# A hybrid attention and recurrent trunk in float32 pairs: gate products, weight casts and the last turn of the recurrent layer rearranged

## The chip, the cores and the metric

The kernel runs on one core of one Trainium2 chip. The metric is the device time of one execution in microseconds (us), as the median of several runs.

## The reference

The reference is an encoder trunk of two layers over 1040 tokens (16 meta tokens and 1024 of the sequence) of width 1024. Layer 0 is attention with a SiLU gate; the change leaves it alone. Layer 1 is recurrent, and it is where everything here happens:

```
zp = rms_norm(h) @ w_in;  u, gate = split(zp)        # 2048 columns each
xc = conv_b + sum(up[tap:tap+T] * conv_w[tap] for tap in 0..3)
for each direction (forward, backward):
    r = sigmoid(xc @ w_a + b_a);  i = sigmoid(xc @ w_x + b_x)     # 16 blocks of 128 x 128
    log_a = -8 * r * softplus(-lam);  a = exp(log_a)
    b = sqrt(1 - exp(2 * log_a)) * i * xc
    h_t = a_t * h_(t-1) + b_t
y = (forward + backward) * silu(gate);   out = h + y @ w_out
```

## The kernel before

**Number format.** Every matrix product is made of three: each operand is held as a rounded part ("hi", fp32r) and a remainder ("lo"), and lo times hi, hi times lo and hi times hi are added in PSUM. For a weight, `split_w` loads the raw 128x512 tile (SP's queue, tile wr, 3 buffers), makes the rounded half on GpSimd (line 106, tile wh) and the remainder on GpSimd (line 107, tile wl; 4 buffers of each). These three are issued at a priority 200 instructions ahead of where they stand. The weights of the recurrent gates have tiles of their own (wown).

**The recurrent layer.** Rows of the 2048 channels are cut into 16 blocks of 128 channels, one turn of the loop for each (line 1300, e = 0 to 15). Three blocks are in work in one turn: `cur` is projected (three chunks `u_chunk` of 346 to 348 columns and two chunks `g_chunk` of 512, each of 24 matmuls), `prev` has its four gate products (`gate(d, j)`: direction d, j = 0 for r and 1 for i; 9 matmuls for d = 0 and 6 for d = 1), its decays and its square root, and `late` has its two scans and is stored to HBM (s_y for the rounded part, s_yl for the remainder). PSUM has three single banks for the chunks (tag c), one tile of three banks (big, gates of d = 0) and one of two (two, gates of d = 1).

The names in the profile: pu and pg are the chunks' PSUM tiles, pz those of the gate products; ou the projected row, oxc the convolved row (lines 1166 to 1169), oxh and oxl its two halves (lines 758, 759); tz the tanh of r, then the decay's root; oz the tanh of i, then i times xc, then the recurrence's input and its result; oa the decay; og the half gate argument, otg its SiLU; oyh and oyl the halves of y.

**Order.** The framework's scheduler turns the program's order into one in-order queue for each engine, by priorities and an estimate of its own of when operands are ready. So the text order below is a wish and not the queue.

**After the loop.** The last block's gates and scans are finished, blocks 0 to 13 of y are read back from HBM (`y_load`, lines 1283 and 1284, two transfers of 512 KB for a block), and the output product runs over 8 tiles of 128 rows (d), each in four quarters of the 16 blocks (`o_part(d, qd)`, 24 matmuls of 512 columns, PSUM tile oo). Tiles 0, 1 and 2 are accumulated at the same time; the others one after another.

Of the kernel before, what the change touches and what calls it, by code (L numbers as in the profile page):

```python
# [10 lines left out]
AF = mybir.ActivationFunctionType  # L11
ALU = mybir.AluOpType
# [5 lines left out]
T = 1040  # L18
NM = 16
# [22 lines left out]
def trunk_kernel(ctx: ExitStack, tc: tile.TileContext, a: dict, out: bass.AP):  # L42
# [51 lines left out]
    def split_w(src, shape, nm, own=None, eng=nc.gpsimd, own_bufs=1):  # L94
        n = 1
        for s in shape:
            n *= s
        raw = wpool.tile([P, 512], F32, tag="wr", name="wr", bufs=3)
        if own:
            hi, lo = [sb["P"].tile([P, 512], F32R, tag=own + z, name="wown", bufs=own_bufs) for z in "hl"]  # L100
        else:
            hi = wpool.tile([P, 512], F32R, tag="wh", name="wh", bufs=4)
            lo = wpool.tile([P, 512], F32R, tag="wl", name="wl", bufs=4)
        with tc.high_priority(sb.get("ahead", 200)):
            nc.sync.dma_start(raw[:, :n], src)
            eng.tensor_scalar(hi[:, :n], raw[:, :n], 1.0, 1.0, ALU.mult, ALU.mult)  # L106
            eng.tensor_sub(lo[:, :n], raw[:, :n], hi[:, :n].bitcast(F32))  # L107
        if len(shape) == 2:
            f = lambda t: t[:, :n].rearrange("p (k m) -> p k m", k=shape[0])
        else:  # L110
            f = lambda t: t[:, :n]
        return f(hi), f(lo)
# [1033 lines left out]
    class Lru:  # L1146
# [25 lines left out]
            self.c = split(self.xc, "ox", "X")  # L1172

        def g_in(self, c, t):
            if c == 0:
                self.og = row("og", "T")
            nc.vector.scalar_tensor_tensor(self.og[:, 512 * c:512 * c + 512], t, 0.5, rstd[:, CHR[c][0]:CHR[c][1]],
                                           ALU.mult, ALU.mult)

        def g_chunk(self, c, w):  # L1180
            t = bank("pg", "c")
            chunk_mm(w, (0, 1), t, *CHR[c])
            self.g_in(c, t)

        def g_last(self, w):

            ts = [bank("pg", "c") for _ in range(2)]
            for hf in range(2):
                for c in range(2):
                    chunk_mm(w, (hf,), ts[c], *CHR[c])  # L1190
            for c in range(2):
                self.g_in(c, ts[c])

        def silu(self):
            og = self.og
            tg = self.tg = row("otg", "T")
            nc.scalar.activation(tg[:, :1024], og[:, :1024], AF.Tanh)
            nc.vector.scalar_tensor_tensor(tg[:, :1024], tg[:, :1024], 1.0, og[:, :1024], ALU.add, ALU.mult)

        def weights(self):  # L1200
            self.w = w_gates(self.e)
# [1 line left out]
        def gate(self, d, j):  # L1203
# [9 lines left out]
            mm3(ps, P, [(gh[:, 2 * d + j], gl[:, 2 * d + j], *self.c)], ch, off, True, True)  # L1213
            if j == 0 and d == 0:
                self.tz = sb["P"].tile([P, 2, T], F32, tag="tz", name="tz", bufs=2)
            z = self.tz[:, d] if j == 0 else row("oz", "X")
            bc = hb[:, 32 * j + 16 * d + e:32 * j + 16 * d + e + 1]
            nc.scalar.activation(z[:, :n], src, AF.Tanh, scale=0.5, bias=bc)
            if j == 1:
                self.z[d] = z  # L1220
                nc.vector.scalar_tensor_tensor(z[:, :n], z[:, :n], 1.0, self.xc[:, T - n:T], ALU.add, ALU.mult)

        def decay(self, d):

# [21 lines left out]
        def scan(self, d):  # L1246
            ti, av, n = self.z[d], self.av[d], T if d == 0 else T - NM
            if d == 0:
                nc.vector.tensor_tensor_scan(ti, av, ti, 0.0, ALU.mult, ALU.add)
            else:  # L1250
                nc.vector.tensor_tensor_scan(ti[:, :n][:, ::-1], av[:, :n][:, ::-1], ti[:, :n][:, ::-1], 0.0,
                                             ALU.mult, ALU.add)
                nc.gpsimd.tensor_add(ti[:, :1024], self.z[0][:, NM:T], ti[:, :1024])  # L1253

        def gated(self):
            yv = self.z[1]
# [42 lines left out]
    w_u = w2_load(0, 1)  # L1299
    for e in range(16):  # L1300
        cur = Lru(e)
        w_g = w2_load(e, 0)
        if e == 0:
            raw = [bank("pu", "c") for _ in range(3)]
# [21 lines left out]
        else:  # L1326
# [2 lines left out]
            cur.u_chunk(0, w_u)  # L1329
            if late:  # L1330
                late.scan(0)
            prev.gate(0, 0)
            prev.decay(0)
            cur.u_chunk(1, w_u)
            if late:
                late.scan(1)
            prev.gate(1, 0)
            prev.decay(1)
            cur.u_chunk(2, w_u)
            cur.conv()  # L1340
            prev.root()
            prev.gate(0, 1)
            if e < 15:
                w_u = w2_load(e + 1, 1)
            if late:
                late.gated()
            if e < 15:
                cur.g_chunk(0, w_g)
                cur.split_xc()
                prev.gate(1, 1)  # L1350
                cur.g_chunk(1, w_g)
            else:
                prev.gate(1, 1)
                cur.split_xc()
                cur.g_last(w_g)
            if late:
                late.store()
        cur.silu()
        cur.weights()
        late, prev = prev, cur  # L1360

    def pair_of(nm):
        ts = [bank(nm, "c") for _ in range(2)]
        return [(ts[j], 512 * j, 512 * j + 512) for j in range(2)]

    for e in range(4):
        y_load(e, "H")
    late.drive()
    late.scan(0)
    for d in range(2):  # L1370
        prev.gate(d, 0)
    for d in range(2):
        prev.gate(d, 1)
    for d in range(2):
        prev.decay(d)
    prev.root()
# [5 lines left out]
        y_load(e, "H")  # L1382
    late.store()
    prev.finish()
    o_part(0, 1, acc[0])
    for d in (1, 2):
        o_part(d, 0, acc[d])
    for e in range(8, 14):
        y_load(e, "X")
    for d in (1, 2):  # L1390
        o_part(d, 1, acc[d])
    for qd in range(2, 4):
        for d in range(3):
            o_part(d, qd, acc[d])
            if qd == 3:
# [109 lines left out]
```

## Time and profile before

| | us |
|---|---|
| median of 3 runs | 1940.13 |
| lowest and highest run | 1939.22, 1945.82 |
| the profiled execution | 1936.07 |
| span of its instructions | 1934.3 |
| TensorE busy in the span | 1828.5 |
| VectorE busy | 1278.4 |
| ScalarE busy | 827.9 |
| GpSimd busy | 943.9 |
| granted clock of TensorE, mean | 0.986 |

PE is TensorE's matmuls, PEld its weight loads, DVE is VectorE, ACT ScalarE, POOL GpSimd and SP the engine whose queue issues the transfers. Times of a window are counted from the first instruction. The recurrent loop's matmuls lie between about 1238 and 1725 us, what follows the loop between 1725 us and the end. An engine's busy time in a stretch has its waits left out; the clock is TensorE's granted share of full speed.

### The profile page before, as it was taken

How to read it: one execution, taken by the hardware profiler on the slowest of the kernel's cores; microseconds unless marked ns; L12 is line 12 of the kernel's file. 1: busy time of each engine (PE TensorE's matmuls, PEld its weight loads, DVE VectorE, ACT ScalarE, POOL GpSimd, SP SyncE). 2: the span in 40 equal slices, each digit the busy share in tenths (PEclk: the TensorE clock that was granted, in tenths of full speed). 3: DMA queues.
4: the chain of work that ended last, by engine and by line, in shares of the span. 5: the costliest groups of instructions: out<-in, count | busy, mean ns of one | idle time of the engine just before them, and what ended most of it. 6: DMA issues, size and time to landing. Idle time of an engine off the chain costs nothing.

```text
span 1934.3 us, 28455 instructions
## 1 busy us (share of the span) xinstructions
PE 1828.5 (95%) x10822; PEld 1659.4 (86%) x10822; DVE 1278.4 (66%) x1953; ACT 827.9 (43%) x1366; POOL 943.9 (49%) x780
## 2 busy tenths in 40 slices
PE   8999989998999999999999999999999899988999
PEld 7988988888999999788878999988888788876887
DVE  7686358787663432889888753368898989893000
ACT  5455224444342201666666642155656464652000
POOL 5455355535224652544433333358676777655331
PEclk9999999999999999999999999999999999998999
DMA  5256532222223451323221014312222222246521
GB/s 180 73 184 232 132 84 65 64 75 72 78 75 122 143 194 57 113 73 92 69 70 55 18 47 160 106 50 71 82 67 81 84 69 88 66 157 232 183 82 44
DMA packets 111062, 192.77 MB, mean 100 GB/s; under 512 B 32143, under 2 KB 51727, under 8 KB 110926
## 3 DMA queue, kind: packets, MB, share of 16 engines
q1 hardware_dynamic: 110926, 190.96, 31.4%
q8 instruction: 85, 1.39, 0.3%
q14 instruction: 51, 0.42, 0.1%
HBM read 129.86 MB, written 53.06 MB: 95 GB/s over the span
## 4 chain that ended last, share of the span: by engine, by line
PE 53%; DVE 20%; POOL 9%; issue 9%; DMA 5%; ACT 4%; SPq 1%; DVEq 0%; ACTq 0%; POOLq 0%
PE pj L159 10%; PE oo L159 8%; PE pxop L159 6%; PE px L918 4%; PE av L998 4%; PE op L159 3%; PE up L159 3%; PE tp L982 3%; PE vps L426 2%; DVE tz L1243 2%; DMA wr<-in_wg 2%; POOL oz L1253 2%; POOL wl L107 2%; DVE oxc L1167 2%; PE pg L1143 2%
## 5 line engine op out<-in xcount | busy, mean ns | idle before, releaser
L106 POOL TENSOR_SCALAR wh<-wr 128x512 fp32r<-128x512 f32 (+2 forms) x219 | 196.3, 897 | 396.4 <-PE pj L159 99.0
L107 POOL TENSOR_TENSOR wl<-wr,wh 128x512 fp32r<-128x512 f32 (+2 forms) x219 | 352.6, 1610 | 17.5
L159 PE MATMUL pj<-xh,wl 128*128 128x346 f32 (+1 forms) x768 | 251.8, 328 | 12.3 <-DVE wl L107 7.2
L159 PE MATMUL pj<-xl,wh 128*128 128x346 f32 (+1 forms) x768 | 249.3, 325 | 0.7 <-DVE xl L260 0.6
L159 PE MATMUL pj<-xh,wh 128*128 128x346 f32 (+1 forms) x768 | 248.9, 324 | 0.0
L159 PEld LDWEIGHTS pj<-xh,wl 128*128 128x128 f32 x768 | 146.6, 191 | 14.2 <-ACT xh L259 7.1
L159 PEld LDWEIGHTS pj<-xl,wh 128*128 128x128 f32 x768 | 146.7, 191 | 2.2 <-DVE xl L260 2.1
L159 PEld LDWEIGHTS pj<-xh,wh 128*128 128x128 f32 x768 | 146.6, 191 | 0.1
L936 POOL TENSOR_SCALAR mpm<-p,mmx 128x96 f32<-128x96 f32 (+1 forms) x69 | 25.7, 372 | 209.2 <-DVE mmx L931 119.9
L1143 PE MATMUL pu<-h1h,wl 128*128 128x346 f32 (+1 forms) x384 | 125.5, 327 | 0.8 <-POOL wh L106 0.8
L1143 PE MATMUL pu<-h1l,wh 128*128 128x346 f32 (+1 forms) x384 | 124.9, 325 | 0.0
L1143 PE MATMUL pu<-h1h,wh 128*128 128x346 f32 (+1 forms) x384 | 124.8, 325 | 0.0
L988 ACT CAST pth<-tp 128x512 fp32r<-128x512 f32 (+1 forms) x160 | 78.9, 506 | 83.4 <-PE tp L982 82.0
L1294 DVE TENSOR_TENSOR hres<-oo,hres 128x512 f32<-128x512 f32 x16 | 10.6, 687 | 151.6 <-PE oo L159 151.6
L989 DVE TENSOR_TENSOR ptl<-tp,pth 128x512 fp32r<-128x512 f32 (+1 forms) x160 | 91.9, 583 | 23.3 <-ACT pth L988 21.7
L159 PE MATMUL oo<-oyl,wh 128*128 128x512 f32 x256 | 102.3, 400 | 4.4 <-DMA oyl<-s_yl 4.4
L159 PE MATMUL oo<-oyh,wl 128*128 128x512 f32 x256 | 100.3, 401 | 3.3 <-DMA oyh<-s_y 3.3
L159 PE MATMUL oo<-oyh,wh 128*128 128x512 f32 x256 | 102.7, 402 | 0.0
L1143 PE MATMUL pg<-h1h,wl 128*128 128x512 f32 x256 | 101.4, 396 | 0.0
L1143 PE MATMUL pg<-h1h,wh 128*128 128x512 f32 x256 | 101.1, 395 | 0.0
L1143 PE MATMUL pg<-h1l,wh 128*128 128x512 f32 x256 | 100.8, 394 | 0.0
L982 PE MATMUL tp<-ident,p 128*128 128x128 f32 (+1 forms) x576 | 96.2, 274 | 0.0
(446 smaller groups left out, 5564.5 us busy)
## 6 DMA issues: line engine op xcount, KB each, us to landing
wr<-in_w SPq DMA_DIRECT2D x128, 256.0 KB
wr<-in_wo SPq DMA_DIRECT2D x64, 256.0 KB
s_y<-oyh SPq DMA_DIRECT2D x14, 512.0 KB
s_yl<-oyl SPq DMA_DIRECT2D x14, 512.0 KB
oyh<-s_y SPq DMA_DIRECT2D x14, 512.0 KB
oyl<-s_yl SPq DMA_DIRECT2D x14, 512.0 KB
s_g<-gth SPq DMA_DIRECT2D x10, 520.0 KB
xr<-in_x SPq DMA_DIRECT2D x8, 520.0 KB
```

The source lines that it names most:

```text
L106: eng.tensor_scalar(hi[:, :n], raw[:, :n], 1.0, 1.0, ALU.mult, ALU.mult)
L107: eng.tensor_sub(lo[:, :n], raw[:, :n], hi[:, :n].bitcast(F32))
L159: nc.tensor.matmul(t[:, :c1 - c0], w, x[:, c0:c1], start=first and j == 0 and pi == 0, stop=last and j == nt - 1 and pi == 2)
L426: nc.tensor.matmul(ps[:m, :n], s, w, start=j == 0 and pi == 0, stop=j == nt - 1 and pi == 2)
L918: nc.tensor.matmul(dst[:m, d0:d0 + a1 - a0], l[:, s], r[:, a0:a1], start=pi == 0, stop=pi == 4)
L982: nc.tensor.transpose(tp[:, o:o + m], p_[:m, NM + P * (kt + j):NM + P * (kt + j) + P], ident[:m, :m])
L988: nc.scalar.copy(hi[:, :w], tp[:, :w])
L989: nc.vector.tensor_sub(lo[:, :w], tp[:, :w], hi[:, :w].bitcast(F32))
L998: nc.tensor.matmul(av[:, :n], l[:, vs], pts[kt][o][:, j * n:j * n + n], start=kt == 0 and j == 0 and pi == 0, stop=False)
L1143: nc.tensor.matmul(t[:, :c1 - c0], l, r[:, c0:c1], start=hf == 0 and k == 0 and pi == 0, stop=hf == 1 and k == 3 and pi == 2)
L1167: nc.vector.scalar_tensor_tensor(xc[:, 2:T], u[:, 0:T - 2], cw[0], xc[:, 2:T], ALU.mult, ALU.add)
L1243: nc.vector.scalar_tensor_tensor(tz[:, d, :n], av[:, :n], 1.0, tz[:, d, :n], ALU.add, ALU.mult)
```

## The change

All of it is in the recurrent layer and after it.

- `split_w` can make the rounded half of a weight on ScalarE (`nc.scalar.copy`) instead of GpSimd. This is on for the loads issued in turns 1 to 15, and off before and after.
- `gate(d, 1)`: the tanh of i is written back into its PSUM tile, and VectorE reads it from there. Before, it went to the row oz in SBUF.
- `g_in`: the half gate argument is written back into the chunk's PSUM bank, ScalarE takes the tanh of each 512 columns from there, and VectorE's product for the SiLU reads the bank. Before, both chunks went to a row og in SBUF and one tanh and one product of 1024 columns followed at the turn's end (`silu`, which is gone).
- `scan(1)`: the sum of the two directions is made by VectorE instead of GpSimd.
- The order in a turn: each gate product stands one product later, the root after the first gate chunk, the load of the next u weights before the root.
- Turn 15: one gate product stands between the two halves of the last gate projection.
- After the loop: the late block's `drive` and first scan stand after the last block's gates, and quarter 1 of the output product is done for tiles 0 to 2 after quarter 0 of all three, as quarters 2 and 3 were before.

```diff
@@ split_w
-            eng.tensor_scalar(hi[:, :n], raw[:, :n], 1.0, 1.0, ALU.mult, ALU.mult)
+            if sb.get("hi_act"):
+                nc.scalar.copy(hi[:, :n], raw[:, :n])
+            else:
+                eng.tensor_scalar(hi[:, :n], raw[:, :n], 1.0, 1.0, ALU.mult, ALU.mult)
@@ class Lru
         def g_in(self, c, t):
             if c == 0:
-                self.og = row("og", "T")
-            nc.vector.scalar_tensor_tensor(self.og[:, 512 * c:512 * c + 512], t, 0.5, rstd[:, CHR[c][0]:CHR[c][1]],
-                                           ALU.mult, ALU.mult)
+                self.tg = row("otg", "T")
+            tg = self.tg[:, 512 * c:512 * c + 512]
+            nc.vector.scalar_tensor_tensor(t, t, 0.5, rstd[:, CHR[c][0]:CHR[c][1]], ALU.mult, ALU.mult)
+            nc.scalar.activation(tg, t, AF.Tanh)
+            nc.vector.scalar_tensor_tensor(tg, tg, 1.0, t, ALU.add, ALU.mult)
...
-        def g_last(self, w):
+        def g_last(self, w, between):
             for hf in range(2):
                 for c in range(2):
                     chunk_mm(w, (hf,), ts[c], *CHR[c])
+                if hf == 0:
+                    between()
...
-        def silu(self):
-            og = self.og
-            tg = self.tg = row("otg", "T")
-            nc.scalar.activation(tg[:, :1024], og[:, :1024], AF.Tanh)
-            nc.vector.scalar_tensor_tensor(tg[:, :1024], tg[:, :1024], 1.0, og[:, :1024], ALU.add, ALU.mult)
...
-            z = self.tz[:, d] if j == 0 else row("oz", "X")
-            nc.scalar.activation(z[:, :n], src, AF.Tanh, scale=0.5, bias=bc)
-            if j == 1:
-                self.z[d] = z
-                nc.vector.scalar_tensor_tensor(z[:, :n], z[:, :n], 1.0, self.xc[:, T - n:T], ALU.add, ALU.mult)
+            if j == 0:
+                nc.scalar.activation(self.tz[:, d, :n], src, AF.Tanh, scale=0.5, bias=bc)
+            else:
+                z = self.z[d] = row("oz", "X")
+                nc.scalar.activation(src, src, AF.Tanh, scale=0.5, bias=bc)
+                nc.vector.scalar_tensor_tensor(z[:, :n], src, 1.0, self.xc[:, T - n:T], ALU.add, ALU.mult)
...
-                nc.gpsimd.tensor_add(ti[:, :1024], self.z[0][:, NM:T], ti[:, :1024])
+                nc.vector.tensor_add(ti[:, :1024], self.z[0][:, NM:T], ti[:, :1024])
@@ the loop
+        sb["hi_act"] = e > 0
...
             cur.u_chunk(0, w_u)
             if late:
                 late.scan(0)
-            prev.gate(0, 0)
-            prev.decay(0)
             cur.u_chunk(1, w_u)
             if late:
                 late.scan(1)
+            prev.gate(0, 0)
+            prev.decay(0)
+            cur.u_chunk(2, w_u)
+            cur.conv()
             prev.gate(1, 0)
             prev.decay(1)
-            cur.u_chunk(2, w_u)
-            cur.conv()
-            prev.root()
-            prev.gate(0, 1)
-            if e < 15:
-                w_u = w2_load(e + 1, 1)
             if late:
                 late.gated()
             if e < 15:
+                w_u = w2_load(e + 1, 1)
                 cur.g_chunk(0, w_g)
+                prev.root()
+                prev.gate(0, 1)
                 cur.split_xc()
-                prev.gate(1, 1)
                 cur.g_chunk(1, w_g)
             else:
-                prev.gate(1, 1)
+                prev.root()
                 cur.split_xc()
-                cur.g_last(w_g)
+                cur.g_last(w_g, lambda: prev.gate(0, 1))
+            prev.gate(1, 1)
             if late:
                 late.store()
-        cur.silu()
@@ after the loop
+    sb["hi_act"] = False
     for e in range(4):
         y_load(e, "H")
-    late.drive()
-    late.scan(0)
     for d in range(2):
         prev.gate(d, 0)
     for d in range(2):
         prev.gate(d, 1)
+    late.drive()
+    late.scan(0)
...
-    o_part(0, 1, acc[0])
     for d in (1, 2):
         o_part(d, 0, acc[d])
     for e in range(8, 14):
         y_load(e, "X")
-    for d in (1, 2):
-        o_part(d, 1, acc[d])
-    for qd in range(2, 4):
+    for qd in range(1, 4):
         for d in range(3):
             o_part(d, qd, acc[d])
```

## Rows read from the trace of the kernel before

**Rows 1.** Windows, turn by turn (engines' busy us, clock, DMA share, GB/s)

```profile
1344.96:1376.30 31.34, 28.10 (x149) 24.72 (x148) 28.85 (x21) 18.00 (x16) 21.87 (x13) 1.00 0.23 76
1376.30:1407.66 31.36, 28.83 (x145) 25.54 (x144) 28.86 (x22) 18.00 (x16) 21.41 (x13) 0.95 0.23 76
```

**Rows 2.** DVE's groups by shape, 1330 to 1690 us: busy, mean ns, idle before

```profile
L1221 DVE SCALAR_TENSOR_TENSOR oz<-oz,oxc 128x1024 f32<-128x1024 f32 x11 | 37.5, 3408 | 0.0
...
L1257 DVE TENSOR_TENSOR oz<-oz,otg 128x1024 f32<-128x1024 f32 x12 | 19.5, 1624 | 29.9 <-POOL oz L1253 29.9
...
L1221 DVE SCALAR_TENSOR_TENSOR oz<-oz,oxc 128x1040 f32<-128x1040 f32 x11 | 16.4, 1494 | 0.0
...
L1198 DVE SCALAR_TENSOR_TENSOR otg<-otg,og 128x1024 f32<-128x1024 f32 x12 | 15.7, 1312 | 0.0
```

**Rows 3.** Chain of waits in time order, third turn (start us, us, what)

```profile
1291.86 3.81 PE pu L1143 x24
1295.66 1.42 PE pz L119 x9
...
1300.91 1.40 PE pz L119 x6
...
1307.57 5.61 PE pg L1143 x24
```

**Rows 4.** Three VectorE lines, whole span: ns min/median/max, first and last start

```profile
L1159 DVE TENSOR_TENSOR ou<-pu,rstd x45: 500/505/518, 1272.0 to 1715.9; 128x346 f32<-128x346 f32 x30, 128x348 f32<-128x348 f32 x15
L1177 DVE SCALAR_TENSOR_TENSOR og<-pg,rstd x32: 662/677/692, 1262.6 to 1732.0; 128x512 f32<-128x512 f32 x32
L1221 DVE SCALAR_TENSOR_TENSOR oz<-oz,oxc x32: 1212/1648/3452, 1282.7 to 1746.0; 128x1040 f32<-128x1040 f32 x16, 128x1024 f32<-128x1024 f32 x16
```

**Rows 5.** POOL's groups by shape, 1330 to 1690 us

```profile
L107 POOL TENSOR_TENSOR wl<-wr,wh 128x512 fp32r<-128x512 f32 x46 | 100.4, 2182 | 3.8
L106 POOL TENSOR_SCALAR wh<-wr 128x512 fp32r<-128x512 f32 x46 | 56.9, 1236 | 9.7 <-PE pg L1143 9.7
L1253 POOL TENSOR_TENSOR oz<-oz 128x1024 f32<-128x1024 f32 x12 | 28.9, 2407 | 66.1 <-DVE tz L1235 66.1
...
L106 POOL TENSOR_SCALAR wown<-wr 128x512 fp32r<-128x512 f32 x12 | 11.3, 938 | 12.5 <-DMA wr<-in_wg 12.5
```

**Rows 6.** ACT's groups by shape, 1330 to 1690 us

```profile
L1197 ACT ACTIVATE otg<-og 128x1024 f32<-128x1024 f32 x11 | 11.7, 1063 | 48.5 <-DVE og L1177 48.5
L758 ACT CAST oxh<-oxc 128x1040 fp32r<-128x1040 f32 x11 | 11.7, 1060 | 76.4 <-DVE oxc L1169 76.4
```

**Rows 7.** PE's waits, 1300 to 1700 us: total us, times, longest

```profile
PE pz L119 <- DVE oxl L759: 14.9, 11, 1.5
```

**Rows 8.** Windows after the loop's last chunk

```profile
1725.00:1731.00 6.00, 0.52 (x2) 0.55 (x3) 6.00 (x6) 1.68 (x2) 3.03 (x2) 0.89 0.88 331
1731.00:1741.00 10.00, 10.00 (x39) 8.29 (x38) 10.00 (x7) 5.62 (x6) 2.95 (x1) 0.72 0.72 262
...
1751.00:1767.00 16.00, 12.63 (x42) 9.75 (x42) 12.01 (x7) 0.51 (x1) 8.63 (x4) 0.81 0.52 201
1767.00:1786.00 19.00, 17.72 (x69) 13.95 (x70) 1.23 (x1) 0.54 (x1) 7.60 (x8) 0.91 0.77 282
1786.00:1930.00 144.00, 143.71 (x620) 116.14 (x620) 9.56 (x15) 0.00 (x0) 42.15 (x44) 1.00 0.33 109
```

**Rows 9.** All waits, 1700 to 1800 us

```profile
POOL oz L1253 <- DVE oz L1251: 6.7, 1, 6.7
...
PE pz L119 <- issue: 5.8, 1, 5.8
...
PE oo L159 <- DMA oyl<-s_yl: 4.4, 2, 3.2
...
PE oo L159 <- DMA oyh<-s_y: 3.3, 1, 3.3
```

**Rows 10.** SP's queue on the timeline after the loop (start, us held)

```profile
1736.60 10.98 SPq L105 DMA_DIRECT2D wr<-in_wo  x2
```

## The prediction

> **What bounds the kernel now.** The reader should take the stretches first, because the limit is not the same in and after the loop. In the windows cut turn by turn, a turn takes 31.3 us (two of twelve stand in [rows 1]; ten of the others lie between 31.1 and 31.4, the last one, at the loop's end, is 30.3). VectorE is busy 28.85 us of it. The groups of VectorE say where the rest is: the product with the SiLU (line 1257) idles 29.9 us in 12 turns, 2.49 us in each, for GpSimd's sum of the two directions, and no other group in [rows 2] has idle time. 28.85 + 2.49 = 31.34 is the whole turn. So VectorE sets the loop's pace, with one wait in its queue.
>
> TensorE, busy 28 to 30 us by the same windows, is not at its own pace. An undisturbed turn shows what it needs [rows 3]: three u chunks of 3.82, two gate products of 1.42 and two of 1.40, two g chunks of 5.61, together 28.3 us. It loses 3.0 us a turn: a wait for the remainder of xc before the first gate product (14.9 us in 11 turns, [rows 7]), a similar one for its rounded half, and a clock that falls to 0.95 of full in some turns [rows 1].
>
> VectorE's operations are stretched. The same form of line 1221 takes 1.21 us at best and 3.45 at worst [rows 4], and its second call averages 3.41 [rows 2], the call that on the timeline has GpSimd's remainder of y beside it. The operations that read PSUM, lines 1159 and 1177, stay within 500 to 518 and 662 to 692 ns in all their calls [rows 4], although GpSimd is busy 70% of the turn [rows 1]. So an operation with both operands in SBUF pays for GpSimd's work, one with an operand in PSUM does not.
>
> After the loop TensorE is the bound from 1786 on: 620 matmuls in 143.7 us, 0.232 each, at clock 1.00 [rows 8]. Before that it stalls. It ends the last chunk at 1724.7 (1731 less the 0.52 us of work in that window and less the 5.8 us wait of [rows 8, 9]). Up to 1786 are 61.3 us, in which it does the last block's four gate products (5.64) and 768 - 620 = 148 matmuls (34.3): 21.3 us are lost. They are the wait of 5.8 and the low clock behind it (0.72 over 10 us: 2.8), then waits of 3.3 and 4.4 for the blocks of y [rows 9] and the low clock around them (0.81 over 16 us and 0.91 over 19: 4.7), in all 21.0.
>
> The loop's loss: from 1291.86 [rows 3] to 1724.7 are 14 turns, 432.8 us, against 14 x 28.3 = 396.2. **36.6 us in the loop and 21.3 behind it** are all that there is to win; the sum is made against the profiled 1936.07.
>
> **The change part by part: VectorE in a turn.**
> - The sum on VectorE: the wait of 2.49 goes, and an operation of 1024 columns with both operands in SBUF comes. It costs 1.21 (best of line 1221, [rows 4]) to 1.62 (line 1257, [rows 2]); I take 1.3.
> - SiLU: a product of 1.31 goes [rows 2], and two of 512 columns with a PSUM operand come, 0.677 each as line 1177 [rows 4]: +0.04. The first product only writes to PSUM instead of SBUF; no row shows that write. I take the same 0.677, as the operation is the same but for the place of its result. Below, it can't be less than the 0.66 of the best call; above, I let it double, 1.35, and the +1.3 of two of them leads into rival 2.
> - i times xc from PSUM: lines 1159 and 1177 give 0.506 for 348 columns and 0.677 for 512, so 1.23 for 1040. The two calls cost 1.49 + 3.41 now: 2.44 less. But what stretched them is GpSimd's work, which then meets other operations: between 0 and 2.44 is kept; I take half, 1.2, as GpSimd's remainder of y stays.
> - GpSimd loses the sum and five casts, 4 x 1.24 + 0.94 = 5.9 of its 21.9 us [rows 5, 1]. The cast's share of VectorE's stretching is between nothing and 5 x 0.62 = 3.1 (0.62 is half the mean, taken as a cast's own time without its waits). I take half, 1.55.
>
> Sum: 28.85 + 1.3 + 0.04 - 1.2 - 1.55 = 27.4, with ends 24.6 (28.85 + 1.21 + 0.04 - 2.44 - 3.1) and 30.5 (28.85 + 1.62 + 0.04 and no relief). At 27.4 VectorE is below TensorE's 28.3, and TensorE becomes the bound.
>
> [...]
>
> **ScalarE.** It is busy 18.0 us a turn [rows 1]. Five casts of 512 columns come. A cast of 1040 takes 1.06 [rows 6]; half of that to the whole is 0.53 to 1.06, I take 0.55, 2.75 a turn. The tanh in two halves adds some 0.2. ScalarE stands at 21 of 28.3 us and has its longest idle times where the casts can go: 76.4/12 = 6.4 us a turn before oxh and 48.5/12 = 4.0 before the SiLU's tanh [rows 6]. So the casts cost nothing while they stand there. Without that cover they cost their 2.75, and the waits that GpSimd has ahead of them now, 9.7/12 = 0.8 for TensorE's release of wh and 12.5/12 = 1.0 for the gate weights' transfer [rows 5]; behind them in ScalarE's queue stand the tanhs of the gates and the convolution's first step, for which VectorE waits.
>
> **TensorE in a turn.** The first gate product comes one chunk (3.8 us) later against a wait of at most 1.5 to 2, so that wait and the half clock behind it go. The banks are held longer: a g bank now waits for a tanh and a second product. With three banks the first is wanted again after a g chunk, two gate products and a u chunk, 12.2 us, against 0.68 + 0.6 + 0.68 of work: free. Gate tiles are wanted again after more than 10 us too. The u weights' load is moved ahead of a root and a gate product: two transfers, their casts and remainders; SP holds them anyway until the raw buffers come free, so nothing.
>
> New in VectorE's queue are waits for ScalarE's tanh (twice in g_in). I put 0.6 us a turn on them and take a turn of 28.9 us; bounds 28.3 and 30.5. Thirteen turns from 1291.86 at 28.9 and the last at 28.3 lose 7.8 of the 36.6: **28.8 us gained in the loop** (36.6 at the lower bound, 8.0 at the upper: 13 x 2.2 = 28.6 lost).
>
> **After the loop.** Between the last u chunk and the last block's gates stand 15.4 us of matmuls (one gate product of 1.4 more than the 14.0 now), and VectorE's queue up to oxl is shorter by 2.49 - 1.3. So the wait of 5.8 falls to about 2.5 to 3, and part of the low clock with it: 3 to 8.6 of 8.6, I take 5. Quarter 1 of tile 0 now needs blocks 4 to 7 after one part of 24 x 0.232 = 5.6 us; then after three, 16.7. The loads of four blocks (4.2 MB) need 12.7 us at the 331 GB/s of [rows 8]. SP also stood 10.98 us before weights [rows 10] while GpSimd, which makes their remainders, waited 6.7 us in its queue for the scan [rows 9]; that sum has left GpSimd. I take 8 of the 12.4 us (bounds 0, if the loads are only late elsewhere, and 12.4). **13 us gained**, between 3 and 21.
>
> **Rivals.**
> 1. VectorE remains the bound: the stretching only moves from operation to operation. That it is an exclusive meeting of the two engines' work, and GpSimd's remainders (2.18 each, five a turn) stay, speaks for it; that PSUM readers are immune speaks against. A turn of 30.0 to 30.5 gives 14.5 to 8 in the loop, and behind it come 13 to 3: 1909 to 1925, about 1916.
> 2. New waits for ScalarE in VectorE's queue take the place of the one removed: four tanhs of which none was on its path at the turn's end. VectorE at the upper 30.5 plus 1.4 of waits is 31.9: a loss of 46.8 against 36.6, the tail's 13 gives it back: 1933, no change.
> 3. Slower: ScalarE's queue becomes the bound. If the casts stand behind its waits instead of in them, its turn is 18.0 + 10.4 (waits of [rows 6]) + 2.75 + 1.8 = 33 us: 13 x 4.7 = 61 lost in the loop against 36.6, less the tail's 13: 1947. It decides from a turn of 32.9; at 32.1 loop and tail cancel. Against it: those waits are for VectorE and shrink with its load.
> 4. The tail gives nothing (loads late at another place): 1907 with the loop as forecast.
>
> **How the numbers follow.** 1936.07 - 28.8 - 13 = 1894.3. The median of the runs is 4 above the profiled one, which leads to 1898; I give 1896, between. Chances: forecast with or without the full tail (rival 4) 0.62, its own range 1883 to 1909; rival 1 0.22; rival 2 0.09; rival 3 0.07. Range 1883 (36.6 + 16.5 gained) to 1926 (rival 1's end). What a measurement here tells from no change is about 0.5%, 9.7 us: faster 0.84, within 0.09, slower 0.07.
>
> **What would show it.** Right: turns of 28.5 to 29.3 in the windows, VectorE 26 to 28.5 busy with no idle behind GpSimd, TensorE at clock 1.00 without a wait before pz, line 1221 at 1.2 to 1.25 in all calls, ScalarE about 21; less than 3 us idle after the last chunk and no wait for y longer than 2. Wrong: turns above 30 with VectorE full (rival 1); VectorE idle behind ScalarE's tanh (rival 2); ScalarE waiting for weights with the tanhs behind it, or TensorE waiting for wh (rival 3); a wait for y moved to quarter 2 (rival 4).

## The result, and the profile after

The changed kernel takes 1924.2 us (median of 4 runs, 1921.69 to 1926.35) against 1939.68 of the kernel before (4 runs): ratio 0.9918, 95% interval 0.9896 to 0.994. It is 15.5 us faster, where 1896 was forecast, 43.7 under the same median. The profiled execution takes 1925.2 with a span of 1923.4, 10.9 shorter than before. From the first chunk of the third turn to the loop's last product it needs 426.5 us instead of 432.8 (6.3 gained), from there to the last matmul 197.4 instead of 205.0 (7.5 gained); the part ahead of the loop, which the change leaves alone, came out 3.0 longer in this execution.

First the windows over two turns, as in [rows 1] (busy us of PE, PEld, DVE, ACT, POOL, then clock, DMA share, GB/s):

```profile
1464.81:1495.90 31.09, 30.39 (x160) 26.80 (x159) 27.36 (x22) 20.71 (x21) 12.76 (x6) 1.00 0.23 83
1495.90:1527.03 31.13, 28.88 (x146) 25.58 (x145) 27.08 (x22) 21.01 (x22) 12.93 (x6) 0.95 0.22 74
```

VectorE is busy 27.1 to 27.4 us instead of 28.85, ScalarE 21, GpSimd 13 instead of 22, all close to the forecast. Yet the turn is 31.1, hardly shorter than 31.3, and nothing is full. VectorE's groups by shape from 1330 to 1690 us, which answer to [rows 2], say what it waits for:

```profile
L1254 DVE TENSOR_TENSOR_SCAN oz<-oa,oz 128x1024 f32<-128x1024 f32 x12 | 35.3, 2943 | 0.4
L1247 DVE TENSOR_TENSOR oz<-oz,tz 128x1024 f32<-128x1024 f32 x12 | 29.5, 2458 | 0.0
L1256 DVE TENSOR_TENSOR oz<-oz 128x1024 f32<-128x1024 f32 x12 | 25.7, 2138 | 0.4
L762 DVE TENSOR_TENSOR oxl<-oxc,oxh 128x1040 fp32r<-128x1040 f32 x11 | 25.6, 2326 | 0.0
...
L1170 DVE SCALAR_TENSOR_TENSOR oxc<-ou,vec,oxc 128x1038 f32<-128x1038 f32 x12 | 15.6, 1300 | 15.9 <-ACT oxc L1169 15.9
...
L1246 DVE SCALAR_TENSOR_TENSOR tz<-oa,tz 128x1040 f32<-128x1040 f32 x11 | 13.7, 1243 | 24.6 <-ACT tz L1239 24.6
```

The wait for GpSimd's sum [rows 2] is gone. In its place stand two for ScalarE: 24.6/11 = 2.24 us a turn for the root (line 1239) and 15.9/12 = 1.33 for the convolution's first step (line 1169). 27.1 + 2.24 + 1.33 = 30.7, and with some 0.3 of small gaps this is the turn. Line 1224, which now reads i from PSUM, is what [rows 4] let expect of such a reader: 1.21 to 1.24 us in all 32 calls, where line 1221 went up to 3.45.

```profile
L1224 DVE SCALAR_TENSOR_TENSOR oz<-pz,oxc x32: 1208/1222/1243, 1292.6 to 1738.7; 128x1040 f32<-128x1040 f32 x16, 128x1024 f32<-128x1024 f32 x16
```

How the two waits come about is seen on the timeline of one turn, ScalarE first (start, us, engine, line, what, in brackets the idle time before it):

```profile
1464.81 1.26 ACT L1169 ACTIVATE oxc<-ou,vec 128x1040 f32<-128x1040 f32 x1 [4.77 <-DVE ou L1162]
1465.97 1.10 ACT L1220 ACTIVATE tz<-pz,hb 128x1024 f32<-128x1024 f32 x1
1467.10 1.25 ACT L1233 ACTIVATE oa<-tz,c1n 128x1024 f32<-128x1024 f32 x1
1468.38 1.25 ACT L1234 ACTIVATE tz<-tz,c1p 128x1024 f32<-128x1024 f32 x1
1469.65 1.28 ACT L1239 ACT_TABLE_LOAD   x1
1470.94 1.94 ACT L1239 ACTIVATE tz<-tz 128x2080 f32<-128x2080 f32 x1
```

and VectorE in the same turn:

```profile
1464.28 0.49 DVE L1162 TENSOR_TENSOR ou<-pu,rstd 128x346 f32<-128x346 f32 x1
...
1466.10 1.30 DVE L1170 SCALAR_TENSOR_TENSOR oxc<-ou,vec,oxc 128x1038 f32<-128x1038 f32 x1 [1.33 <-ACT oxc L1169]
...
1472.92 2.38 DVE L1246 SCALAR_TENSOR_TENSOR tz<-oa,tz 128x1040 f32<-128x1040 f32 x2 [2.24 <-ACT tz L1239]
```

The reader is to see a ring. ScalarE idles 4.77 us with the convolution's first step at the head of its queue, until VectorE has evacuated the last chunk of u. Only behind that step stand the second direction's tanh, the two operations of its decay, the table load and the root, 8.1 us from 1464.81 to 1472.9. VectorE has 4.6 us of work beside them (three convolution steps of 1.30 and one product of 0.69) and idles the other 3.57; then come 23 us of its own up to the next evacuation, for which ScalarE waits again. The chain of waits from 1464 to 1500 (start, us, what) runs through these two engines alone and comes back to its start 31.09 us later:

```profile
1464.81 1.26 ACT oxc L1169
...
1470.94 1.95 ACT tz L1239
1472.92 1.95 DVE tz L1246 x2
...
1495.43 0.45 DVE ou L1162
1495.88 0.03 issue
1495.90 1.26 ACT oxc L1169
```

GpSimd's groups, as in [rows 5], show the casts gone (the rounded half is now ScalarE's, 622 ns each), while its subtractions last as long as before:

```profile
L110 POOL TENSOR_TENSOR wl<-wr,wh 128x512 fp32r<-128x512 f32 x46 | 97.2, 2122 | 168.2 <-ACT wh L107 168.0
```

Behind the loop, all waits from 1700 to 1800, for [rows 9]:

```profile
PE pz L122 <- DVE oz L1224: 4.1, 1, 4.1
...
PE oo L162 <- DMA oyl<-s_yl: 1.9, 1, 1.9
PE oo L162 <- DMA oyh<-s_y: 1.5, 1, 1.5
...
PE oo L162 <- DVE oz L1224: 0.9, 1, 0.9
```

TensorE's wait of 5.8 and the 7.7 for y [rows 9] have become 5.0 for line 1224, which frees the bank in which i is now kept, and 3.4 for y. Of the 5.0, 4.1 are for the block before the last: the tanh and line 1224 of its first i product come so late that the last block's first gate product finds the three-bank tile still taken.

### The profile page after: what moved, and what is told of

It reads as the page before. It is cut to its first block, busy times and chain, and to the rows that moved or that the text cites. A ratio compares the mean times of both kernels' runs of the same rounds, so it can differ in the third digit from the quotient of the medians.

```text
span 1923.4 us, 28579 instructions
## 1 busy us (share of the span) xinstructions
PE 1827.8 (95%) x10822; PEld 1660.2 (86%) x10822; DVE 1260.6 (66%) x1985; ACT 866.7 (45%) x1455; POOL 804.3 (42%) x691
## 3 DMA queue, kind: packets, MB, share of 16 engines
q1 hardware_dynamic: 110926, 190.96, 31.2%
## 4 chain that ended last, share of the span: by engine, by line
PE 53%; DVE 25%; ACT 8%; issue 4%; POOL 4%; DMA 3%; SPq 1%; DVEq 0%; ACTq 0%; POOLq 0%
PE pj L162 11%; PE oo L162 8%; PE pxop L162 6%; PE px L921 4%; PE av L1001 4%; PE op L162 3%; PE up L162 3%; PE tp L985 3%; DVE oz L1247 3%; PE vps L429 2%; DVE oz L1254 2%; DVE oz L1224 2%; DVE oxl L762 2%; PE py L921 2%; DVE oz L1256 2%
## 5 line engine op out<-in xcount | busy, mean ns | idle before, releaser
L110 POOL TENSOR_TENSOR wl<-wr,wh 128x512 fp32r<-128x512 f32 (+2 forms) x219 | 347.1, 1587 | 239.3 <-ACT wh L107 226.4
L109 POOL TENSOR_SCALAR wh<-wr 128x512 fp32r<-128x512 f32 (+2 forms) x160 | 125.7, 786 | 363.6 <-PE oo L162 95.0
L939 POOL TENSOR_SCALAR mpm<-p,mmx 128x96 f32<-128x96 f32 (+1 forms) x69 | 25.6, 371 | 217.4 <-DVE mmx L934 122.2
```

## The experiments

Two theories: (A) the new order makes the ring, and costs what the other parts gain; (B) the gains on VectorE were overestimated, because GpSimd stretches other operations instead.

**e1: the old order in the changed kernel.** Casts, PSUM operands, sum on VectorE and the part after the loop stay. (The lines are shortened here: conditions are left out, a product and its decay stand on one line, and the last turn, which also has its old order again, is not shown.)

```diff
...
             cur.u_chunk(0, w_u)
             late.scan(0)
+            prev.gate(0, 0); prev.decay(0)
             cur.u_chunk(1, w_u)
             late.scan(1)
-            prev.gate(0, 0); prev.decay(0)
-            cur.u_chunk(2, w_u); cur.conv()
             prev.gate(1, 0); prev.decay(1)
+            cur.u_chunk(2, w_u); cur.conv()
+            prev.root(); prev.gate(0, 1)
+            w_u = w2_load(e + 1, 1)
             late.gated()
-            w_u = w2_load(e + 1, 1)
             cur.g_chunk(0, w_g)
-            prev.root(); prev.gate(0, 1)
             cur.split_xc()
+            prev.gate(1, 1)
             cur.g_chunk(1, w_g)
-            prev.gate(1, 1)
...
```

> The changed kernel with the old text order of the turn; everything else of the change stays. Theory A (a ring through two in-order queues): moving the second direction's gate product behind the convolution put that direction's decay and the root behind the convolution's first step in ScalarE's queue, and that step waits for VectorE's last evacuation of u; VectorE, busy 27.1 us a turn, then waits 2.2 us for the root and 1.3 us for the convolution's first step, which makes 31. With the old order the decays stand before that step again, the wait for the root goes and a turn takes 28.6 to 29.4 us: some 1895 to 1905 us in all. Theory B (stretching): VectorE is held by GpSimd's work, its waits for ScalarE only fill a gap that is there anyway, and the turn stays at 30.7 to 31.2: 1921 to 1928.

Measured: 1897.99, ratio 0.979 (0.9773 to 0.9807), 26 us under the changed kernel. The turn is 28.5 to 30.4, on the mean 29.05. VectorE no longer waits for the root, but 28.3/12 = 2.4 us for the convolution's first step, which in ScalarE's queue now stands behind both decays and two casts, and ahead of the root. With the old order the forecast time is met within 2 us.

**e2: the new order alone in the kernel before** (the same moves the other way, all else as before).

> The kernel before with only the new order of the turn and of the last turn. Theory A: the two waits for ScalarE come on top of VectorE's 28.85 us and of the wait for GpSimd's sum, less what of the stretching meets them: a turn of 32.5 to 34.5, 1950 to 1978 us. Theory B: the order only moves work, the turn stays at 31.0 to 31.5: 1930 to 1942.

Measured: 1944.34, ratio 1.0024 (1.0013 to 1.0035). The turn is 31.6 to 32.7, on the mean 32.1 and between the two forecasts; beside the old wait for GpSimd (27.5/11 = 2.5) come 14.6/11 = 1.3 for the convolution's step and 9.7/11 = 0.9 for the root. The ring's two waits appear, but they cost only 5 us: VectorE's busy time fell from 28.85 to 27.2 us a turn beside them. A's price was too high here, its mechanism was not.

**e5: one product back.** A single move in the changed kernel:

```diff
+            prev.gate(1, 0)
+            prev.decay(1)
             cur.u_chunk(2, w_u)
             cur.conv()
-            prev.gate(1, 0)
-            prev.decay(1)
```

> The changed kernel with one gate product moved back: the second direction's first one, with its decay, stands ahead of the third u chunk again; the first direction's stays one product later. In ScalarE's queue only one operation of that decay, instead of the gate's tanh and two, then stands between the convolution's first step and the root. Theory A: the root is ready 5.7 us after the last evacuation of u, when VectorE has done the wait of 1.3, three convolution steps and a gate product (5.9 us), so its wait for the root goes from 2.2 to under 0.5 and that for the convolution's first step stays: a turn of 28.6 to 29.4, 1893 to 1905 us. Theory B' (the later first gate product, or the tanhs of the gate chunks, set the turn): 30.5 or more, 1917 or more.

Measured: 1889.42, ratio 0.9756 (0.9737 to 0.9775). The turn is 28.3. Windows from 1370 to 1690, and VectorE's groups:

```profile
1370.00:1690.00 320.00, 320.00 (x1691) 285.71 (x1690) 295.74 (x251) 229.08 (x236) 128.81 (x70) 1.00 0.28 92
```

```profile
L1170 DVE SCALAR_TENSOR_TENSOR oxc<-ou,vec,oxc 128x1038 f32<-128x1038 f32 x13 | 16.9, 1300 | 23.9 <-ACT oxc L1169 23.9
...
L1246 DVE SCALAR_TENSOR_TENSOR tz<-oa,tz 128x1040 f32<-128x1040 f32 x13 | 16.0, 1232 | 0.4 <-ACT tz L1239 0.4
```

TensorE is busy all 320 us at clock 1.00: the bound forecast for the loop is reached once the second direction's tanh and the first operation of its decay stand ahead of the convolution's step in ScalarE's queue. The second operation, the table load and the root still stand behind it, but VectorE's wait for the root is gone. The wait for the step is even longer (1.84), but VectorE's busy time of 26.15 and this wait are 28.0 together, under TensorE's 28.3.

**e3: the ring opened at its other link.** The convolution's first step on VectorE, all else as changed.

```diff
-                nc.scalar.activation(xc, u, AF.Identity, scale=cw[2], bias=vcol(V_CB + e))
+                nc.vector.tensor_scalar(xc, u, cw[2], vcol(V_CB + e), ALU.mult, ALU.add)
```

> The changed kernel with the convolution's first step (scale and bias of 1040 columns) on VectorE instead of ScalarE. Theory A: VectorE gets 0.65 to 1.25 us more work, but neither waits for that step (1.3) nor for the root (2.2), as the root no longer stands behind a step that VectorE releases: VectorE needs 27.8 to 28.4, TensorE's 28.3 becomes the bound, a turn of 28.4 to 29.0, 1890 to 1902 us. Theory B: the work on VectorE adds up: a turn of 31.5 to 32.3, 1932 to 1942.

Measured: 1889.02, ratio 0.9742 (0.9722 to 0.9761), turn 28.3, TensorE busy throughout. VectorE does 1.12 us more of its own in a turn and still the loop is 2.7 us a turn shorter, since the decays no longer wait for VectorE's evacuation. Only 9.9/13 = 0.8 us of wait for the root is left.

**e9: only gate(1, 0) and its decay late** (e1's kernel with the product of the second direction behind the convolution).

> The kernel of the run with the old text order, with one gate product moved the other way: the second direction's first one and its decay stand behind the third u chunk and the convolution, as in the change; all other products stay in the old places. Theory A: this alone closes the ring. Between the convolution's first step and the root stand then two tanhs, two operations of the decay and the table load: the root is ready 9.2 us after the last evacuation of u, VectorE has 7.1 us of work and wait by then, so it waits 2 us for the root and 1.3 for the convolution's first step again: a turn of 30.2 to 31.2, 1912 to 1928 us. Rival: the loss comes from several moved products together; then a turn of 28.7 to 29.5, 1896 to 1907.

Measured: 1904.03, ratio 0.9807 (0.9789 to 0.9825), turn 29.0. Its VectorE groups:

```profile
L762 DVE TENSOR_TENSOR oxl<-oxc,oxh 128x1040 fp32r<-128x1040 f32 x12 | 14.9, 1243 | 0.0
L1246 DVE SCALAR_TENSOR_TENSOR tz<-oa,tz 128x1040 f32<-128x1040 f32 x12 | 14.9, 1242 | 24.6 <-ACT tz L1239 24.6
```

Theory A missed. Both waits came as it said (2.05 and 1.33), but the turn did not grow to 31, because VectorE was busy only 25.6 us. The two waits alone are not the loss; VectorE's work around them counts too. On the mean e1's turn is just as long (29.05), so this product alone, moved in the old order, costs the loop nothing; the 6 us between the two medians lie outside it.

**e13 and e14: which of the other moves makes the rest.** e13 is the changed kernel with gate(0, 0) and decay(0) back ahead of u chunk 1; e14 has instead the root, gate(0, 1), gate(1, 1) and the load of u weights at their old places.

> The changed kernel with gate(0, 0) and decay(0) back ahead of u chunk 1; gate(1, 0), the root and the others stay late. Together with the next run it divides the 2 us a turn by which the changed kernel (31.05) stands above the kernel with gate(1, 0) alone late (29.0). Theory P (the place of the first direction's product costs them: its tanh and decay come into ScalarE's queue later, and so all behind it): turn 29.0 to 29.6, 1902 to 1910. Theory Q (the root and gate(0, 1) behind the first gate chunk cost them): turn still 30.6 to 31.1, 1917 to 1926. Rival, only together: both this run and the next stand at 29 to 29.5.

> The changed kernel with the root, gate(0, 1) and gate(1, 1) and the u weights' load back at their old places; gate(0, 0) and gate(1, 0) stay one chunk later. The counterpart of the run before. Theory P: turn 30.6 to 31.1, 1917 to 1926. Theory Q: turn about 29.0, 1900 to 1908. Rival, only together: 29 to 29.5 in both.

Measured: e13 1927.7, ratio 0.9945 (0.9928 to 0.9962), turn 31.2; e14 1906.7, ratio 0.9835 (0.9818 to 0.9852), turn 29.6. So it is the group of moves that theory Q names, and not the first direction's first product; but which of the group is told only by the traces, as e14 takes all of them back. It is hardly the root: in ScalarE's queue it stands in both kernels behind the second direction's decay. What moved in VectorE's queue is the product of i and xc for the first direction (line 1224). In e14 VectorE makes it between the convolution's steps, while ScalarE is at the decay:

```profile
1486.69 1.30 DVE L1171 SCALAR_TENSOR_TENSOR oxc<-ou,vec,oxc 128x1039 f32<-128x1039 f32 x1
1487.91 1.24 DVE L1224 SCALAR_TENSOR_TENSOR oz<-pz,oxc 128x1040 f32<-128x1040 f32 x1
1489.06 1.29 DVE L1172 SCALAR_TENSOR_TENSOR oxc<-ou,vec,oxc 128x1039 f32<-128x1039 f32 x1
```

Its tanh makes ScalarE's part longer (9.0 us instead of 8.1 from the convolution's step to the root), so the waits stay almost the same: 2.23 and 1.33 in e13, and 2.07 and 1.33 in e14. What differs is VectorE's busy time, 27.4 against 26.15, and most of that in one group, first of e13, then of e14:

```profile
L762 DVE TENSOR_TENSOR oxl<-oxc,oxh 128x1040 fp32r<-128x1040 f32 x11 | 25.4, 2308 | 0.0
```

```profile
L762 DVE TENSOR_TENSOR oxl<-oxc,oxh 128x1040 fp32r<-128x1040 f32 x12 | 14.9, 1243 | 0.0
```

The timelines show why. In e13 the remainder of xc comes behind line 1224 and starts 0.85 us after a subtraction of GpSimd, whose end it waits for; in e14 it comes earlier and starts 0.5 us ahead of one, and then GpSimd's lasts longer (first e13, then e14):

```profile
1479.38 2.04 POOL L110 TENSOR_TENSOR wl<-wr,wh 128x512 fp32r<-128x512 f32 x1 [0.17 <-ACT wh L107]
1480.23 2.30 DVE L762 TENSOR_TENSOR oxl<-oxc,oxh 128x1040 fp32r<-128x1040 f32 x1
```

```profile
1466.36 1.24 DVE L762 TENSOR_TENSOR oxl<-oxc,oxh 128x1040 fp32r<-128x1040 f32 x1
1466.87 1.89 POOL L110 TENSOR_TENSOR wl<-wr,wh 128x512 fp32r<-128x512 f32 x1 [11.71 <-ACT wh L107]
```

**e15: GpSimd's subtractions of weights away.** They are set to zero, so the remainders' share of the loop's weight products is missing.

```diff
-            eng.tensor_sub(lo[:, :n], raw[:, :n], hi[:, :n].bitcast(F32))
+            if sb.get("hi_act"):
+                eng.memset(lo[:, :n].bitcast(F32), 0.0)
+            else:
+                eng.tensor_sub(lo[:, :n], raw[:, :n], hi[:, :n].bitcast(F32))
```

> The changed kernel with the remainders of the weights that are loaded in turns 1 to 15 set to zero by GpSimd (the subtraction is left out, so the remainders' share of those products is missing; all matrix products still run). It takes away the work of GpSimd that reads two SBUF operands. Theory S (VectorE's busy time in the ring of waits counts, and GpSimd's subtractions stretch it): VectorE's busy time falls from 27.1 to 25.6 or less, the waits of 3.5 stay, turn 29.1 or less, 1905 or less. Rival (the ring is made of waits and ScalarE's time alone): VectorE's busy time falls, its waits grow by as much, turn above 30.5, 1917 or more.

Measured: 1890.62, ratio 0.9753 (0.9737 to 0.9768), turn 28.3 in the changed order. VectorE's groups:

```profile
L765 DVE TENSOR_TENSOR oxl<-oxc,oxh 128x1040 fp32r<-128x1040 f32 x13 | 16.0, 1234 | 0.0
L1259 DVE TENSOR_TENSOR oz<-oz 128x1024 f32<-128x1024 f32 x13 | 15.9, 1226 | 0.4
L1263 DVE TENSOR_TENSOR oz<-oz,otg 128x1024 f32<-128x1024 f32 x13 | 15.8, 1216 | 0.0
```

The sum falls from 2138 to 1226 ns, the remainder of xc from 2326 to 1234, VectorE's busy time from 27.1 to 23.7 (267.75 of 320), and TensorE is busy all 320 us. Waits of 1.5 for the convolution's step and 1.3 for the root are still there (theory S had 3.5 for both) and cost nothing. Theory S holds, and with it B's mechanism as the ring's other half: the loss is 3.6 us of waits in a ring with 3.4 us of stretching, and taking away either restores TensorE's 28.3.

In this trace GpSimd's memsets, which only write, do not stretch the remainder of xc: it has a whole one beside it in most turns, and takes 1234 ns on the mean of 13 calls, where it took 2326 in the changed kernel with the subtractions:

```profile
1464.64 1.23 DVE L765 TENSOR_TENSOR oxl<-oxc,oxh 128x1040 fp32r<-128x1040 f32 x1
1464.98 0.53 POOL L111 MEMSET wown<- 128x512 f32 x1 [0.34 <-PE pz L125]
```

The sum has no memset beside it in most turns; for it the run shows only that it is undisturbed without the subtractions (1226 ns).

**e4, e7, e6, e11: the other parts one by one in the kernel before.** e4 has only the sum on VectorE, e7 only the tanh of i and the SiLU's argument kept in PSUM, e6 only the casts on ScalarE, e11 the edits of e4 and e7 together.

```diff
-                nc.gpsimd.tensor_add(ti[:, :1024], self.z[0][:, NM:T], ti[:, :1024])
+                nc.vector.tensor_add(ti[:, :1024], self.z[0][:, NM:T], ti[:, :1024])
```

> The kernel before with only the sum of the two directions on VectorE. Both theories: the wait of 2.49 us goes and the sum costs 1.2 (undisturbed) to 2.1 us (as it is in the changed kernel): a turn of 30.1 to 30.9, 1920 to 1932 us. It prices this part; if the turn stays at 31.3, another wait took the place.

> The kernel before with only the gate's tanh and the SiLU's argument kept in PSUM. By the prediction's term (half of 2.44 us a turn, less 0.04) a turn of 30.1, 1921 us; if all of the stretching moves to other operations 31.3 and 1936; if none does 28.9 and 1906.

> The kernel before with only the casts of the weights' rounded halves on ScalarE. By the prediction's term (half of the casts' own time leaves VectorE's stretching, 1.55 us) a turn of 29.8, some 1917 us; if the lock only passes to the remainders, 31.3 and 1936; if the casts crowd ScalarE's queue so that the root stands behind the convolution's first step, VectorE waits for the root and for that step: up to 32.5, 1952.

> The kernel before with two parts alone: tanh and SiLU argument kept in PSUM, and the sum on VectorE; old order, casts on GpSimd, old end. VectorE's turn of 28.9 with the first part has 2.7 us of wait for GpSimd's sum in it; the sum costs 1.2 to 2.1 on VectorE: 27.4 to 28.3, below TensorE's need, so a turn of 28.3 to 28.9 and, with the old end, 1890 to 1900 us.

Measured: e4 1909.18, ratio 0.9847 (0.983 to 0.9863); e7 1901.28, 0.9816 (0.9794 to 0.9838); e6 1939.77, 0.9994 (0.9981 to 1.0006); e11 1890.99, 0.9748 (0.9731 to 0.9765). In e4 the turn is 29.4 and VectorE full (319.28 of 320 us), though its sum takes long:

```profile
L1253 DVE TENSOR_TENSOR oz<-oz 128x1024 f32<-128x1024 f32 x13 | 27.8, 2139 | 0.1
```

28.85 + 2.14 would be 31.0. The other operations together became 1.6 us shorter: GpSimd's sum, too, had stretched them, which the forecast did not count. e7 gains 38 us with 2.7 us a turn of waiting for GpSimd still in it; VectorE's busy time falls to 26.4, by 2.45, what the prediction had as its upper bound. e6 gains nothing: the casts' move takes about 1 us a turn of stretching from VectorE, and a wait of 14.6/11 = 1.3 for the convolution's first step, behind ScalarE's casts, comes in its place. e11's turn is 28.3 to 28.7. The gains do not add up: the PSUM operands and the sum already reach TensorE's need, and nothing is left in the loop for the other parts. With the old order the casts even cost: e1, which is e11 with the casts on ScalarE and the new part after the loop, has turns of 29.05 on the mean against 28.4, and VectorE's wait of 2.4 us for the step behind decays and casts.

**e10: e5 with the casts back on GpSimd.**

```diff
-        sb["hi_act"] = e > 0
+        sb["hi_act"] = False
```

> The kernel of the run with the second direction's gate product moved back, with all weights' casts on GpSimd as before the change. If the casts matter once VectorE has air: VectorE gets some 0.9 us a turn of stretching back (28.9 busy a turn against 28.0 in the run with the casts alone) and a turn is 28.8 to 29.3, 1895 to 1903 us. If TensorE's need hides it: 28.3 to 28.5, 1887 to 1893.

Measured: 1890.21, ratio 0.9744 (0.973 to 0.9759): the same as e5. At this bound it is all one who casts.

**e8 and e12: after the loop.** e8 is the kernel before with the changed part after the loop (`drive` and scan behind the last gates, quarter 1 later). e12 is e5's kernel with the last block's i written to SBUF as before.

> The kernel before with only what the change does after the loop: the late block's drive and scan behind the last gates, and quarter 1 for tiles 0 to 2 after quarter 0 of all three. By the prediction 8 of the 12.4 us of waits for the blocks of y and the low clock around them go: 1931 us; the wait of 5.8 us for the last block's split stays. If the loads are only late elsewhere, 1936 to 1940.

> The kernel of the run with the second direction's gate product moved back, and the last block's two input gates written to SBUF again, so that their PSUM tiles come free with the tanh and not with VectorE's product. TensorE's waits for that product after the loop (0.7 and 1.9 us in the run with the convolution's step on VectorE) go: 1 to 3 us, 1886 to 1889 us. If the tiles are taken by the output product later anyway: no difference.

Measured: e8 1935.38, ratio 0.9987 (0.9975 to 0.9998), 2.5 us; e12 1891.99, ratio 0.9754 (0.9739 to 0.9768), no difference from e5. In e8 the waits for y stay (4.1 and 2.1), and one of 3.1 for a weight's remainder comes in. e12 tries only the last block's own i: TensorE's wait of 1.9 for its bank in e5 is gone, but the waits for y are 3.8 instead of 3.0. It does not touch the 4.1 us of the changed kernel, which are for the block before. These are mostly a consequence of the ring: in e5 and e3, which keep i in PSUM alike, that wait is 0.7.

## Why the prediction was wrong

- **What bounds the kernel before.** Right. With VectorE relieved and nothing new in its way, the loop stands at TensorE's 28.3 [rows 3], in six kernels (e3, e5, e10, e11, e12, e15), with TensorE busy in all 320 us from 1370 to 1690.
- **VectorE's sum, 27.4.** Right in total (27.1), but partly by luck, as the terms were off and the errors cancel. The sum costs 2.14, not 1.3: +0.84. Reading i from PSUM saves 4.90 - 2.45 = 2.45 [rows 2], twice the 1.2 taken: half of it had been given away as moving elsewhere. SiLU: 2 x (0.689 + 0.668) - 2 x 0.677 - 1.31 = +0.05, as forecast. The rest, the share of GpSimd's lost casts and sum, is 27.1 - 28.85 - 2.14 - 0.05 + 2.45 = -1.5, where 1.55 was taken for the casts; alone they gave about 1.0 (e6), the sum's departure 1.6 (e4). The prediction names the sum among what GpSimd loses, but its 5.9 us are the casts alone, and it put nothing on the sum's share of the stretching.
- **The failed step: "New in VectorE's queue are waits for ScalarE's tanh (twice in g_in). I put 0.6 us a turn on them".** The waits are 3.57 us a turn, and not for a tanh but for the root and the convolution's first step. The prediction looked at what the tanhs would add to VectorE's queue and costed the reordering for TensorE alone. It knew that VectorE waits for the convolution's first step, but looked only at casts ahead of it. It did not write down what a product moved behind the convolution brings with it on ScalarE: its tanh and the two operations of its decay, and the root that needs them, now stand behind a step that VectorE releases. Before, they stood ahead of it and ScalarE did them while VectorE was at u. e5 shows it with one product moved back: 35 us. The loss needs more than that product: alone in the old order it costs the loop nothing (e9), and with the group around the first direction's i product back, half of the 35 us is gone (e14).
- **TensorE's banks, "free".** TensorE does wait 17.7 us in ten of the turns for a bank that the SiLU's product frees late. In e5 this is gone, with the banks used alike: a consequence of VectorE's lateness, not a cost of its own. For the gate tiles "more than 10 us" was too much at the loop's end: there the three-bank tile is wanted 8.6 us after its product began, and TensorE waits the 4.1 us. The wait for the remainder of xc [rows 7] went, as forecast. The half clock that was to go with it stayed: between 1300 and 1700 us the granted clock falls to 0.50 four times in the kernel before (from 1389 to 1391 among them) and four times in the changed one (from 1393 to 1395 among them), for some 3.3 us each; in e5 it is 1.00 from 1370 to 1690.
- **The loop.** 28.8 us forecast, 6.3 measured: 31.0 a turn in place of 28.9. These 22.5 us are most of the 30.9 by which the profiled execution missed its 1894.3; the tail makes 5.5 of it and the part ahead of the loop 3.0.
- **The tail.** 13 forecast, 7.5 measured. TensorE waits 3.4 us for y instead of 7.7, and the clock beside these waits is 1.00 from 1741 to 1774 and 0.86 from there to 1786, where it was 0.81 and 0.91. The wait of 5.8 became one of 5.0, where 2.5 to 3 was forecast: the wait for the split went, that for the bank of i came. Of this the after-loop part alone gives 2.5 (e8).
- **Rivals.** Rival 2 (new waits for ScalarE in VectorE's queue; 1933, chance 0.09) is what came, at another place of the queue and with a VectorE relieved as forecast: 27.1 + 3.57 instead of 30.5 + 1.4. Rival 1's mechanism is the other half of it (e15): some of the stretching moved, to the remainder of xc (from 1.63 us in the kernel before to 2.33), the second scan (2.33 to 2.94) and the second direction's product with the root (1.22 to 2.46). Its time, 1916, is nearer than the forecast's, but its sign, "VectorE full", did not show. Rival 3 did not: ScalarE is at 21, with 0.62 for a cast of 512 columns and 2 x 0.60 for the SiLU's tanh in halves, which took 1.06 in one piece.
- **What would have shown it.** The queue of ScalarE in the profile of before. There the idle time ahead of the convolution's step (line 1166) is small, because decays and root stand ahead of it; in the changed kernel 69.8/12 = 5.8 us a turn are empty there (first before, then after):

```profile
L1166 ACT ACTIVATE oxc<-ou,vec 128x1040 f32<-128x1040 f32 x12 | 15.1, 1259 | 22.1 <-DVE ou L1159 22.1
```

```profile
L1169 ACT ACTIVATE oxc<-ou,vec 128x1040 f32<-128x1040 f32 x12 | 15.1, 1257 | 69.8 <-DVE ou L1162 69.8
```

The size could be had too. By the same profile the convolution's step, a tanh, two operations of the decay, the table load and the root take 1.26 + 1.10 + 1.25 + 1.25 + 1.28 + 1.95 = 8.1 us of ScalarE. The changed trace has 4.6 us of VectorE's work beside them, and the rest is the wait.

The version to keep is the changed kernel with one product back (e5, 1889.42) or with the convolution's first step on VectorE (e3, 1889.02): 35 us under the changed kernel and 50 under the one before. The simplest is e11, with PSUM operands and sum alone: at 1890.99 its interval does not tell it from these two. Left open is what the lost time after the loop would need (from 1721.4 to 1774.2 are 52.8 us with some 41 of matmuls).

## What to carry to other kernels

When a matrix product is moved, write out for each in-order queue what its consumers bring along, and look for a step in it that another engine releases: work ahead of such a step runs beside the other engine's work, and behind it it can be added to that engine's turn (here 3.57 us). A busy time forecast right does not give the turn; add the waits of the ring that the new queue orders close. When several parts relieve the same engine, try each alone: here the sum and the PSUM operands reach the next bound by themselves (e11), and the reordering then took back 26 us (e1). Moving one product back was enough to undo that (e5), though the same product alone did no harm (e9).

## What the runs showed of the hardware

- The same VectorE sum of 1024 columns from two SBUF operands takes 1225 ns (e3), 1382 (e5) or 2138 (changed kernel), by what GpSimd does beside it (1226 in e15, where its subtractions are left out), while the product of i and xc, with one PSUM operand, stays at 1208 to 1243 in all 32 calls of the changed kernel. Keeping an operand in PSUM is worth more than the undisturbed lengths suggest: 2.45 us a turn for two operations (e7).
- The stretching is mutual, and in the pairs shown under e13 and e14 the one that starts second gets longer, by about what is left of the first. VectorE's remainder grows from 1.24 to 2.30 us where 1.19 of GpSimd's subtraction are left. GpSimd's subtraction takes 1.89 us where 0.73 of VectorE's remainder are left, and 1.30 in its shortest calls. These pairs are what the runs show of the exclusive meeting that rival 1 names and of the lock that stands in the expectation of e6. Losing the casts alone did not shorten the subtractions (2122 ns on the mean, 2182 before); other orders did (1639 in e5).
- Reading from PSUM costs no more than reading two undisturbed SBUF operands (1211 ns for 1024 columns in line 1224 against 1219 for the same kind of operation in line 1246, both of the changed kernel).
